# The sums behind the row forms move from the buffer ring "scc" to the ring "ry"

## The chip, the cores and the metric

The kernel runs on one core of one Trainium2 chip. The metric is the device time of one execution in microseconds (us). Of each kernel three plain runs are shown by their median, and one more execution was recorded by the hardware profiler.

## The reference

A two-layer bidirectional encoder trunk over 256 tokens of width 2048, float32. Every layer is a mixer (attention in two parallel head groups and an output projection) and a gated feed-forward network with a short convolution, each behind a normalisation by the root mean square of the row and with a residual. What matters here is the feed-forward part (`D_FF` = 5632, `CONV_W` = 3):

```python
def conv_ffn(x, w_up, conv_w, conv_b, w_down):
    h = jnp.einsum("bsd,df->bsf", x, w_up)
    g, u = h[..., :D_FF], h[..., D_FF:]
    gp = jnp.pad(g, ((0, 0), (1, 1), (0, 0)))
    g = conv_w[0] * gp[:, :-2] + conv_w[1] * gp[:, 1:-1] + conv_w[2] * gp[:, 2:] + conv_b
    return jnp.einsum("bsf,fd->bsd", jax.nn.gelu(g) * u, w_down)
```

## The kernel before

All matrix products run on TensorE with weights streamed from memory in units of 128 x 1024 float32 (`wunit`). A product of float32 precision is made of three products of a reduced format: each operand is split into a high half (a cast on ScalarE, L231) and a low half (source minus high, VectorE, L234), and high x high, high x low and low x high are added up in one PSUM bank (L195, L196, L197). The names `wh` and `wl` are the halves of the weights, `yT` and `prod` the activations of the up and down projections.

The feed-forward network of a layer is done in two halves (`HALVES`): six, then five up blocks (`up_group`), each of 4 x 128 columns of the gate and the same columns of the other factor, and after each half the down projection over the rows that it produced. An up block walks through 8 units of weights for each of two outputs `x`: units 0 to 3 for both outputs by turns, then units 4 to 7 of the one and of the other.

At unit 3 (`UPK`) of each up block, and at three units of each half's down projection (the list `seven`, 1, 2, 3; fewer in the last one), a 2 x 2 block product is done with seven block products instead of eight (a Strassen-Winograd scheme). It needs sums of weight blocks and sums of activation blocks:

- `column_forms` forms the weight sums. `t1` is the first (L951), of ring "rx". `p1` is its split: two tiles, high and low, that are named `form` and, in the up blocks, come from the ring "scc" (L958). The other weights go into the rings of `wh` and `wl`.
- `seven_products` issues seven triples (L977, L978, L979), in the order p21, p22, p11, p3, p1, p2, p4. Four of them go to banks of their own (b1, b5, b6, b7, the tags "s" and "tp"); the triple with p1 goes to b5.
- `extra_parts`, one tick after unit 3, adds those banks up into four tiles named `sum`: `s1` (L844), `x0` (L845), `x1` (L846) and `y1` (L848). `x0` and `x1` come from the ring "ry". L878 adds them to the output at the end of the block.
- `row_forms` forms the activation sums for a down projection from the finished block of activations. It calls `form_sums`, which takes one tile `sums` and writes four sums into it (L324 to L327), and then splits it into `form` tiles. It runs within `multiplied`, for blocks 1, 2, 3 of each half, hence blocks 1, 2, 3 and 7, 8, 9 of each layer.
- `y_forms` forms the activation sums for the up blocks, once a layer, with the same `form_sums`. Its own tile `yf` comes from "ry".

Two orders matter. `multiplied` of a block is put off (`later`) by two ticks, so that in program order it stands in the next up block, behind its unit 1 and ahead of its unit 3. And the framework plans the order of the instructions on each engine itself: it takes what is ready by its own estimate of times, earlier program order first, except where `keep_in_program_order` binds an instruction. A tile of a tag is given out in program order among the tiles of that tag, and an instruction that needs a buffer waits until all readers of the tile that had it are through. The pool `tmp` has two buffers for each tag used here ("scc", "ry", "rx"); all tiles concerned are 128 x 512 float32 or smaller.

Tiles that take buffers in "scc" in the feed-forward network before the change, in program order within an up block: `sums` (where `row_forms` runs), then p1's high half, then p1's low half. In "ry": `x0`, `x1`.

Of the kernel before, what the change touches and what calls it, by code (L numbers as in the profile page):

```python
# [27 lines left out]
F32 = mybir.dt.float32  # L28
# [5 lines left out]
P = 128  # L34
# [37 lines left out]
def trunk_kernel(ctx: ExitStack, tc, a, out):  # L72
# [7 lines left out]
    tmp = ctx.enter_context(tc.tile_pool(name="tmp", bufs=2))  # L80
# [5 lines left out]
    def nm(s):  # L86
        uid[0] += 1
        return f"{s}_{uid[0]}"
# [141 lines left out]
    def split(dst_h, dst_l, src, pin=False):  # L230
        first = S.copy(dst_h, src)  # L231
        if pin:
            tc.keep_in_program_order(first)
        V.tensor_tensor(dst_l, src, dst_h.bitcast(F32), op=ALU.subtract)  # L234
# [70 lines left out]
    def turned_rows(c, gain, res):  # L305

        z = att.tile([P, 2, 512], F32, name=nm("z"), tag="sc", bufs=1)
        V.transpose(z, h[:, :, c * 512:(c + 1) * 512])
        pf = att.tile([P, 8, P], F32, name=nm("hT"), tag="pt", bufs=2)
        moved(z.rearrange("p t k -> p (t k)"), pf)  # L310

        def tiles():
            for j in range(4):
                res[c * 4 + j] = y_tile(pf.rearrange("p (t j) q -> p j t q", t=2)[:, j], gain, c * 4 + j)
            if res is formed.get("of") and c == UPK // 2:
                y_forms(pf.rearrange("p (t j) q -> p j t q", t=2), gain)
        return tiles

    formed = {}

    def form_sums(a11, a21, a12, a22):

        f = tmp.tile([P, 4, P], F32, name=nm("sums"), tag="scc")
        V.tensor_tensor(f[:, 0], a21, a22, op=ALU.add)  # L324
        V.tensor_tensor(f[:, 1], f[:, 0], a11, op=ALU.subtract)
        V.tensor_tensor(f[:, 2], a11, a21, op=ALU.subtract)
        V.tensor_tensor(f[:, 3], a12, f[:, 1], op=ALU.subtract)  # L327
        return f

    def y_forms(src, gain):  # L330

        y = tmp.tile([P, 2, 2, P], F32, name=nm("yf"), tag="ry")
        for k in range(2):
            S.activation(y[:, k], src[:, UPK % 2 * 2 + k], AF.Copy, scale=gain[:, 2 * UPK + k:2 * UPK + k + 1])
        f = form_sums(*(y[:, k, t] for k in range(2) for t in range(2)))
        form = []
        for x, tag in enumerate(("R", "Rq")):
            high = tmp.tile([P, 2, P], F32R, name=nm("form"), tag="t0")
            low = const.tile([P, 2, P], F32R, name=nm("form"), tag=tag, bufs=1)
            split(high, low, f[:, 2 * x:2 * x + 2])  # L340
            form += [(high[:, k], low[:, k]) for k in range(2)]
        formed["form"] = form
# [113 lines left out]
    def qk_tiles(srcs, act, rs, orders, slot):  # L456

        return [qk_sum(ps, r, order, slot + x)
                for x, (ps, r, order) in enumerate(zip(gemm_b(srcs, act), rs, orders))]
# [454 lines left out]

    def row_forms(c4, parts):

        f = form_sums(*(c4[:, 2 + k, t * P:(t + 1) * P] for k in range(2) for t in range(2)))
        form = []
        for high, low in parts:
            n = high.shape[1]  # L920
            split(high, low, f[:, len(form):len(form) + n])
            form += [(high[:, x], low[:, x]) for x in range(n)]
        return form

    def multiplied(j, sides, prod, forms, g0, seven):

        u4, c4 = sides[1], sides[2]
        V.tensor_tensor(c4, c4, u4, op=ALU.mult)
        if j - g0 in seven:
            forms[2 * (j - g0) + 1] = row_forms(c4, new_forms(g0, seven.index(j - g0)))  # L930
        for i in range(4):
            y = new_act("prod", (4 * j + i) % NACT)
            split(y[:, 0, :], y[:, 1, :], c4[:, i, :])
            prod.append(y)
# [223 lines left out]
    for hh in range(2):  # L1158
        vt = v_tiles(gemm_a(a["od_v"][hh], yT, KT), rstd, ((18, 19, 20, 21), (16, 17, 22, 23))[hh])
        for hd in range(hh * 4, hh * 4 + 4):  # L1160
            y = att.tile([P, 6, 64], F32, name=nm("nb"), tag="bias", bufs=2)
# [8 lines left out]
            q, k = qk_tiles([a["od_qk"][hd * 2 + x] for x in range(2)], yT, (Rq, R), (rev, None), hd % 2 * 2)  # L1170
# [236 lines left out]
```

## Time and profile before

| | |
|---|---|
| three runs, median (lowest, highest) | 2412.46 us (2407.63, 2412.59) |
| the profiled execution, its time | 2409.76 us |
| its span, first to last instruction | 2407.9 us |
| mean granted TensorE clock | 0.999 of full speed |
| busy in the span | TensorE matmul 2387.8 us, VectorE 1860.2, ScalarE 1374.0, GpSimd 538.8 |
| HBM read | 458.48 MB |

PE is TensorE's matmuls, PEld its weight loads, DVE VectorE, ACT ScalarE, POOL GpSimd, SP the engine that issues the weight transfers. Rows ordered by time give the start, the duration, the engine, the line, the operation and "output <- inputs" by the names of the tiles, and at the end the number of instructions that the row stands for; a bracket at its end is the idle time of that engine just before, and what ended it. Matmuls are pipelined: one takes 0.39 us, and the next starts about 0.23 us after it did.

### The profile page before, as it was taken

The page shows a single profiled execution, that of the slowest core. Times are in us where ns is not written, and L with a number is a line of the kernel's source. Part 1 is how long each engine was busy: PE and PEld are TensorE (multiplying, and loading weights), DVE is VectorE, ACT ScalarE, POOL GpSimd, SP SyncE. Part 2 cuts the span into 40 slices and gives each one's busy share as a digit, 9 for nine tenths or more (in the row PEclk, how much of TensorE's full clock was granted, in tenths as well). Part 3 has the DMA queues.
Part 4 walks back from the last instruction along what each step waited for, and adds up shares of the span by engine and source line. Part 5 has one row for each costly group of instructions (what it writes and reads, how often), then busy time and mean ns, then how long its engine had stood idle before and what let it go on. Part 6 is the DMA issues. An engine that isn't in the chain of part 4 may idle for free.

```text
span 2407.9 us, 32958 instructions
## 1 busy us (share of the span) xinstructions
PE 2387.8 (99%) x10895; PEld 1982.4 (82%) x10895; DVE 1860.2 (77%) x2461; ACT 1374.0 (57%) x1954; POOL 538.8 (22%) x940
## 2 busy tenths in 40 slices
PE   9999999999999999999999999999999999999998
PEld 7888888888888888888788888888888888888787
DVE  6576567666778888778889868676788887788887
ACT  7455455566656565445656657555565654456564
POOL 1132033322222422004232100422223320033220
PEclk9999999999999999999999999999999999999999
DMA  8778678766777877668777764667778876687874
GB/s 309 203 195 239 196 196 239 216 201 184 218 200 221 213 214 217 202 206 219 213 217 211 221 201 138 193 197 211 201 214 225 208 227 195 207 219 209 236 212 156
DMA packets 287531, 505.64 MB, mean 210 GB/s; under 512 B 159096, under 2 KB 160504, under 8 KB 287360
## 3 DMA queue, kind: packets, MB, share of 16 engines
q1 hardware_dynamic: 256848, 470.15, 65.0%
q0 software_dynamic: 30080, 32.74, 8.0%
q8 instruction: 85, 1.39, 0.2%
q14 instruction: 86, 0.70, 0.1%
q10 hardware_dynamic: 432, 0.66, 0.1%
HBM read 458.48 MB, written 2.18 MB: 191 GB/s over the span
## 4 chain that ended last, share of the span: by engine, by line
PE 45%; DVE 3%; DMA 1%; issue 1%; ACT 1%; SPq 0%; POOL 0%; DVEq 0%; ACTq 0%
PE gm L197 12%; PE gm L196 12%; PE gm L195 12%; PE gm L145 2%; PE gm L150 1%; DVE wl L234 1%; PE gm L978 1%; PE gm L979 1%; PE gm L977 1%; PE tp L978 1%; DVE form L234 1%; DMA qk<-z 1%; ACT wh L231 1%; PE tp L979 0%; PE s L979 0%
## 5 line engine op out<-in xcount | busy, mean ns | idle before, releaser
L231 ACT CAST wh<-raw 128x1024 fp32r<-128x1024 f32 (+1 forms) x897 | 935.7, 1048 | 820.7 <-PE gm L197 651.5
L234 DVE TENSOR_TENSOR wl<-raw,wh 128x1024 fp32r<-128x1024 f32 (+1 forms) x897 | 1085.1, 1216 | 391.3 <-ACT wh L231 384.1
L195 PE MATMUL gm<-wh,yT 128*128 128x512 f32 x2092 | 816.1, 390 | 0.0
L196 PE MATMUL gm<-wl,yT 128*128 128x512 f32 x2092 | 814.7, 389 | 0.3 <-DVE wl L234 0.3
L197 PE MATMUL gm<-wh,yT 128*128 128x512 f32 x2092 | 814.6, 389 | 0.0
L197 PEld LDWEIGHTS gm<-wh,yT 128*128 128x128 f32 x2092 | 392.6, 188 | 82.2 <-DVE yT L240 0.2
L196 PEld LDWEIGHTS gm<-wl,yT 128*128 128x128 f32 x2092 | 392.8, 188 | 81.8 <-DVE wl L234 1.4
L195 PEld LDWEIGHTS gm<-wh,yT 128*128 128x128 f32 x2092 | 392.8, 188 | 80.9 <-ACT junk L265 0.4
L273 POOL DMA_DIRECT2D qk<-sc x264 | 151.7, 583 | 863.9 <-issue 389.6
L273 POOL DMA_DIRECT2D qk<-z x392 | 225.6, 584 | 257.7 <-DVE z L279 227.2
L195 PE MATMUL gm<-wh,prod 128*128 128x512 f32 x518 | 201.5, 389 | 0.0
L197 PE MATMUL gm<-wh,prod 128*128 128x512 f32 x518 | 201.5, 389 | 0.0
L196 PE MATMUL gm<-wl,prod 128*128 128x512 f32 x518 | 201.5, 389 | 0.0
L195 PEld LDWEIGHTS gm<-wh,prod 128*128 128x128 f32 x518 | 97.2, 188 | 20.3
L196 PEld LDWEIGHTS gm<-wl,prod 128*128 128x128 f32 x518 | 97.2, 188 | 20.2
L197 PEld LDWEIGHTS gm<-wh,prod 128*128 128x128 f32 x518 | 97.2, 188 | 20.2
L196 PE MATMUL gm<-wl,mix 128*128 128x512 f32 x256 | 100.1, 391 | 0.9 <-DVE wl L234 0.9
L195 PE MATMUL gm<-wh,mix 128*128 128x512 f32 x256 | 100.0, 391 | 0.0
L197 PE MATMUL gm<-wh,mix 128*128 128x512 f32 x256 | 99.6, 390 | 0.0
L273 POOL DMA_DIRECT2D hT<-z x72 | 41.4, 583 | 199.8 <-PE gm L197 75.5
L856 ACT ACTIVATE sum<-sum,rstd 128x512 f32<-128x512 f32 x88 | 59.7, 718 | 17.7 <-DVE sum L845 10.0
L145 PE MATMUL gm<-yT,wh 128*128 128x512 f32 x256 | 59.5, 390 | 0.0
(356 smaller groups left out, 2644.1 us busy)
## 6 DMA issues: line engine op xcount, KB each, us to landing
raw<-in_up SPq DMA_DIRECT2D x352, 512.0 KB, 4.5
raw<-in_down SPq DMA_DIRECT2D x176, 512.0 KB, 4.4
raw<-in_eva_qk SPq DMA_DIRECT2D x96, 512.0 KB, 4.3
raw<-in_eva_v SPq DMA_DIRECT2D x46, 512.0 KB, 6.0
raw<-in_evb_qk SPq DMA_DIRECT2D x32, 512.0 KB, 4.7
raw<-in_ev_out SPq DMA_DIRECT2D x32, 512.0 KB, 4.3
raw<-in_od_qk SPq DMA_DIRECT2D x32, 512.0 KB, 4.3
raw<-in_od_out SPq DMA_DIRECT2D x32, 512.0 KB, 4.3
```

Of the source, the lines that this page charges most:

```text
L145: T.matmul(ps.rearrange("p a b -> p (a b)"), wh[:, k * P:(k + 1) * P], act[u * 8 + k].rearrange("p a b -> p (a b)"), start=(u == 0 and k = ...
L150: T.matmul(ps[:, 1, :], wl[:, k * P:(k + 1) * P], act[u * 8 + k][:, 0, :], start=False, stop=(u * 8 + k == KT - 1))
L195: T.matmul(ps[t], ah, wh[:, sl], start=(kt == 0), stop=False)
L196: T.matmul(ps[t], ah, wl[:, sl], start=False, stop=False)
L197: T.matmul(ps[t], al, wh[:, sl], start=False, stop=(kt == nk - 1))
L231: first = S.copy(dst_h, src)
L234: V.tensor_tensor(dst_l, src, dst_h.bitcast(F32), op=ALU.subtract)
L273: (nc.sync if i in on_sync else G).dma_start(dst[j * 32:(j + 1) * 32, :, i * 32:(i + 1) * 32], z[i * 32:(i + 1) * 32].rearrange("p (b j c) ...
L856: S.activation(sums[x][t], sums[x][t], AF.Copy, scale=rstd[0][:, t:t + 1])
L977: T.matmul(ps, ah, wh, start=own and first, stop=False)
L978: T.matmul(ps, ah, wl, start=False, stop=False)
L979: T.matmul(ps, al, wh, start=False, stop=own and last)
```

## The change

`form_sums` gets the ring as an argument. `y_forms` passes "scc" as before; `row_forms` passes "ry", so that its `sums` tile takes a buffer from the ring of `x0` and `x1` and not from that of p1. The rest of the code is the same.

```diff
-    def form_sums(a11, a21, a12, a22):
+    def form_sums(tag, a11, a21, a12, a22):
 
-        f = tmp.tile([P, 4, P], F32, name=nm("sums"), tag="scc")
+        f = tmp.tile([P, 4, P], F32, name=nm("sums"), tag=tag)
...
     def y_forms(src, gain):
...
-        f = form_sums(*(y[:, k, t] for k in range(2) for t in range(2)))
+        f = form_sums("scc", *(y[:, k, t] for k in range(2) for t in range(2)))
...
     def row_forms(c4, parts):
 
-        f = form_sums(*(c4[:, 2 + k, t * P:(t + 1) * P] for k in range(2) for t in range(2)))
+        f = form_sums("ry", *(c4[:, 2 + k, t * P:(t + 1) * P] for k in range(2) for t in range(2)))
```

## The prediction

> **What bounds the kernel now.** I read the page first, then the table of waits for TensorE, then the time-ordered lists of TensorE, VectorE and ScalarE around one up block that stalls and one that doesn't.
>
> ```profile
> span 2407.9 us, 32958 instructions
> PE 2387.8 (99%) x10895; PEld 1982.4 (82%) x10895; DVE 1860.2 (77%) x2461; ACT 1374.0 (57%) x1954; POOL 538.8 (22%) x940
> ```
>
> TensorE (PE) sets the time: only 2407.9 - 2387.8 = 20.1 us of the span is not matmul. A change that touches no matmul can win only what TensorE waits for. The waits of TensorE (total us, times, longest):
>
> ```profile
> PE tp L978 <- DVE form L234: 8.0, 11, 1.2
> PE gm L196 <- DVE wl L234: 1.2, 2, 0.9
> ```
>
> The first row is the change's place. L978 is the second product of a triple in `seven_products`; "tp <- form" is the fifth triple, whose weight is `p1`, the split of `t1`. TensorE waits 11 times for the low half of p1 (`form` by L234, VectorE). Now the same stretch in a block that doesn't wait (block 1 of layer 0):
>
> ```profile
> 720.65 0.39 PE L977 MATMUL gm<-wh,yT 128*128 128x512 f32 x1
> 723.39 0.40 PE L977 MATMUL tp<-form,form 128*128 128x512 f32 x1
> 723.63 0.39 PE L978 MATMUL tp<-form,form 128*128 128x512 f32 x1
> 723.86 0.40 PE L979 MATMUL tp<-form,form 128*128 128x512 f32 x1
> 725.70 0.39 PE L196 MATMUL gm<-wl,yT 128*128 128x512 f32 x1
> 728.19 0.39 PE L195 MATMUL gm<-wh,yT 128*128 128x512 f32 x1
> ```
>
> and in the next block, which waits:
>
> ```profile
> 763.55 0.39 PE L977 MATMUL gm<-wh,yT 128*128 128x512 f32 x1
> 766.30 0.40 PE L977 MATMUL tp<-form,form 128*128 128x512 f32 x1
> 767.91 0.39 PE L195 MATMUL gm<-wh,yT 128*128 128x512 f32 x1
> 769.35 0.49 PE L978 MATMUL tp<-form,form 128*128 128x512 f32 x1 [1.05 <-DVE form L234]
> 769.68 0.39 PE L979 MATMUL tp<-form,form 128*128 128x512 f32 x1
> 769.91 0.39 PE L196 MATMUL gm<-wl,yT 128*128 128x512 f32 x1
> 772.43 0.39 PE L195 MATMUL gm<-wh,yT 128*128 128x512 f32 x1
> ```
>
> From the first L977 to the last row stand 33 matmuls in both. The undisturbed block takes 728.19 - 720.65 = 7.54 us (0.229 a matmul), the other 772.43 - 763.55 = 8.88. So the stall costs 1.33 us, more than the 1.05 of the wait table, because matmuls overlap and the pipe must fill again. In the bad block the written order has already put seven other matmuls between L977 and L978 of p1, and TensorE still waits.
>
> Where p1 is made. VectorE and ScalarE (ACT) in the undisturbed block:
>
> ```profile
> 711.24 0.61 ACT L231 CAST form<-t 128x512 fp32r<-128x512 f32 x1
> 715.75 0.69 DVE L234 TENSOR_TENSOR form<-t,form 128x512 fp32r<-128x512 f32 x1
> ```
>
> and in the stalled one:
>
> ```profile
> 746.94 1.40 DVE L878 SCALAR_TENSOR_TENSOR z<-gm,rstd,sum 128x512 f32<-128x512 f32 x2
> 752.01 0.69 DVE L951 TENSOR_TENSOR t<-raw 128x512 f32<-128x512 f32 x1 [1.28 <-DMA raw<-in_up]
> 764.65 0.28 DVE L324 TENSOR_TENSOR sums<-qk 128x128 f32<-128x128 f32 x1
> 767.14 0.42 DVE L234 TENSOR_TENSOR form<-sums,form 128x256 fp32r<-128x256 f32 x1
> 767.48 1.22 DVE L234 TENSOR_TENSOR wl<-raw,wh 128x1024 fp32r<-128x1024 f32 x1
> 768.61 0.68 DVE L234 TENSOR_TENSOR form<-t,form 128x512 fp32r<-128x512 f32 x1
> 769.21 0.68 DVE L845 TENSOR_TENSOR sum<-sum,tp 128x512 f32<-128x512 f32 x1
> 770.94 0.68 DVE L846 TENSOR_TENSOR sum<-sum,s 128x512 f32<-128x512 f32 x1
> ```
> ```profile
> 761.42 1.05 ACT L231 CAST wh<-raw 128x1024 fp32r<-128x1024 f32 x1 [1.55 <-DVE raw L955]
> 763.64 1.33 ACT L231 CAST prod<-qk 128x256 fp32r<-128x256 f32 x4 [1.16 <-DVE qk L928]
> 764.87 0.62 ACT L231 CAST form<-t 128x512 fp32r<-128x512 f32 x1
> ```
>
> Undisturbed, p1's halves are written 9.4 and 4.9 us before the seven products start. In the stalled block `t` is there at 752.70, yet p1's high half is cast at 764.87, 1.3 us after the start, although ScalarE stood idle 1.55 and 1.16 us before that. It comes right behind the first write of `sums` (L324, 764.65), and p1's low half at 768.61, behind the last reader of `sums` (767.14 + 0.42). That is the picture of ring "scc": two buffers, and `sums`, p1 high, p1 low ask for them in this order. p1 high can't take its buffer before `sums` took one, and p1 low takes the one that `sums` gives up. The same picture stands in exactly 12 of the 22 up blocks: those behind blocks 1, 2, 3, 7, 8, 9 of each layer, where `row_forms` runs. The other 10 show no wait.
>
> The loss of each of the 12 by the count of 33 matmuls (8.88 us in the first, 9.56 in the last, whose rows follow, each less 7.545): 1.33, 1.24, 1.07, 1.04, 0.66, 0.84, 0.50, 0.40, 1.55, 0.88, 0.70, 2.02. Sum **12.2 us**, the ceiling (the last holds TensorE's 0.3 us wait for `wl` there too).
>
> ```profile
> 2266.24 0.39 PE L977 MATMUL gm<-wh,yT 128*128 128x512 f32 x1
> 2275.80 0.40 PE L195 MATMUL gm<-wh,yT 128*128 128x512 f32 x1
> ```
>
> **The change part by part.** No instruction, byte or DMA is added or removed; no queue (SP, POOL) gets another step. Three dependences change.
>
> 1. p1 no longer shares a ring with `sums`. Its buffers were last read by the previous block's fifth triple (723.86 + 0.40 in the pair above), some 28 us before it wants them. So p1 can be made as in the undisturbed blocks, and TensorE's wait goes: at most 12.2 us.
>
> 2. `sums` now waits for a buffer of "ry", held by the two sums x0 and x1 of the previous `extra_parts` until L878 has read them. L878 ends at 746.94 + 1.40 = 748.34, `sums` is first written at 764.65: 16 us to spare. Cost 0.
>
> 3. x1 (written by L846) now waits until `sums` is read out. That is at 767.56, L846 starts at 770.94: 3.4 us to spare. Cost 0. If that cover went, VectorE would stand at L846 with the next low weights queued behind it; TensorE would wait for those.
>
> What is late next. ScalarE's cast (0.62) moves into its idle time. VectorE's part of p1 moves ahead of the row-form work, and there VectorE is full:
>
> ```profile
> 720.65:728.20 7.55, 7.55 (x35) 6.20 (x34) 7.51 (x11) 6.16 (x10) 0.00 (x0) 1.00 0.78 226
> 763.55:771.10 7.55, 6.50 (x29) 5.02 (x28) 7.55 (x17) 7.37 (x13) 0.00 (x0) 1.00 0.62 176
> ```
>
> (columns: PE, PEld, VectorE, ScalarE busy us; VectorE 7.55 of 7.55.) So everything from there to the first unit behind the seven products (call it U4) moves back by p1 low's share, 0.60 us (768.61 to 769.21), unless VectorE had an idle gap. U4's low weights are wanted 22 matmuls after the start, 5.02 us (725.70 - 720.65 = 5.05 undisturbed). They end now at 5.15 us in the first stalled block (767.48 + 1.22 - 763.55) and 4.98 in the last; in the others between 3.37 and 4.85. With 0.60 added they overrun 5.02 by 0.73, 0.43, 0.09, 0.25 and 0.56 us in five of the 12 blocks, in sum 2.06; with VectorE's gaps just before (0.55 in the second of these, 0.17 in the fourth) about 1.5. Each such wait also refills the pipe: L978 to L979 above took 0.33 where 0.23 is usual, 0.1 apiece, 0.5. So I take 2.0 us as left. Low end: nothing but the 0.13 of the first block is left, if p1 low finds gaps everywhere. High end: the split of `sums`, which in eight blocks stands behind U4's low weights, goes ahead of them because ScalarE reaches its cast 0.5 us sooner; a further 0.60 in those blocks makes 3.9, with refills 4.7. In the last block:
>
> ```profile
> 2270.00 1.22 DVE L234 TENSOR_TENSOR wl<-raw,wh 128x1024 fp32r<-128x1024 f32 x1
> 2271.13 0.69 DVE L234 TENSOR_TENSOR form<-sums,form 128x512 fp32r<-128x512 f32 x1
> ```
>
> Sum: 12.2 - 2.0 = **10.2 us** gained, between 7.5 and 12.1. Against the profiled execution's 2409.76 (span 2407.9 and 1.86 around it) that is 2399.6. The median of the three runs, 2412.46, stands 2.7 above that execution, so I forecast 2402.3 (0.42% faster); the runs themselves spread over 5 us, which is also why 0.2%, 4.8 us, is about what a measurement can tell.
>
> **A rule weighed.** The two rows of stretches above (7.51 of 7.55 and 7.55 of 7.55) say that VectorE has no room there. The Trainium skill, Perfetto Trace Analysis, Identifying Performance Opportunities, says that a kernel generally improves by improving its most-contended engine. VectorE gets no less work here, so by that sentence the stall would stay and the time with it, 2412. The trace speaks against it: in all 12 blocks the late instruction is one whose input was ready about 12 us before (752.70 against 764.87 above), and the undisturbed block has as full a VectorE (7.51 of 7.55) and no wait. That VectorE is full I have charged as the 2.0 us.
>
> **The rivals.**
> - The gain is handed over: VectorE's backlog is worse than the sum says (0.15 to 0.2 us in each of the 12 blocks beyond the high end above, as by `prod` splits in another order). 12.2 - 4.7 less 1.8 to 2.4 leaves 5 to 6 us: 2407. Against it: the ten undisturbed blocks keep U4 ahead.
> - Nothing changes: p1's place is set by the written order, not by the ring, and the new order leaves it behind the row forms; or VectorE's work, not a buffer, is the bound, and the wait only changes its name. Time 2412. For it: VectorE is full. Against it: ScalarE's idle 1.55 and 1.16 us while p1's input lay ready.
> - Slower: x0 and x1 (L845, L846) are written ahead of U4's low weights. They stand before them in program order. x0 needs the sixth triple, which starts 15 matmuls in and ends at about 17 x 0.229 + 0.39 = 4.3 us; then x0 and x1 (0.60 each) and the low weights (1.22) end at 6.7, 1.7 us past 5.02, where the average loss now is 1.0. In 12 blocks 12 x 1.7 - 12.2 = 8 us slower: 2420.7. x0 alone ahead gives 1.1 us a block, no change; it decides from the second sum on. Against it: in every up block of this trace L845 stands behind U4's low weights (767.48 before 769.21 above).
>
> **How the numbers follow.** The forecast (gain 7.5 to 12.2) gets 0.72, handed over 0.10, no change 0.11 (0.07 by the written order, 0.04 by VectorE's work), slower 0.07. Faster by over 0.2% is the first two, 0.82. The lowest run less the ceiling, 2407.6 - 12.2 = 2395.4, is the low end; with handed over at 2407 and a run's spread the range reaches to 2408, and leaves out about 0.2. The likeliest case's own range is 2395.4 to 2405.
>
> **What would show it.** Right: the row "PE tp L978 <- DVE form" is gone; in all 12 blocks p1 low is written 4 to 5 us before the first L977, and L977, L978, L979 of p1 run in a row; the 33 matmuls take 7.5 us except in the first and last block of a half, where "PE gm L196 <- DVE wl" shows some 0.5 us; L846 shows no wait. Wrong: p1's cast still behind the prod casts; or new waits of L196 that add up to several us; or L845 before U4's low weights.

## The result and the profile after

| | before | after |
|---|---|---|
| median of five runs (lowest to highest) | 2412.46 us (2407.63 to 2413.59) | 2402.37 us (2400.53 to 2403.41) |
| the profiled execution | 2409.76 us | 2402.49 us |
| its span | 2407.9 us | 2400.6 us |

The ratio after to before is 0.996, with a 95% interval of 0.9945 to 0.9974: faster. The medians differ by 10.1 us, the two profiled executions by 7.3. The forecast of 2402.3 lies so near partly by luck: it was a gain of 10.2 taken off a median that stood 2.7 above its own profiled execution, and after the change the profiled execution stands at the median. In the later comparisons the median of the kernel before was 2410.0 and 2409.9 us; a forecast made from those would have been 2399.8.

What TensorE waited for, after (total us, times, longest):

```profile
PE gm L196 <- DVE wl L234: 2.5, 5, 0.9
PE tp L978 <- DVE wl L234: 0.6, 1, 0.6
```

The row "PE tp L978 <- DVE form L234: 8.0, 11" is gone. L196 waits 2.5 us where it waited 1.2: 1.3 us of it in three of the 12 blocks (0.3 before), the rest in the mixer of layer 1. The block whose loss was 1.33 us, VectorE's rows after (in order of time):

```profile
752.37 0.69 DVE L951 TENSOR_TENSOR t<-raw 128x512 f32<-128x512 f32 x1 [1.51 <-DMA raw<-in_up]
760.14 0.69 DVE L234 TENSOR_TENSOR form<-t,form 128x512 fp32r<-128x512 f32 x1
765.49 0.28 DVE L324 TENSOR_TENSOR sums<-qk 128x128 f32<-128x128 f32 x1
767.30 0.75 DVE L234 TENSOR_TENSOR form<-sums,form 128x256 fp32r<-128x256 f32 x2
768.31 2.35 DVE L234 TENSOR_TENSOR wl<-raw,wh 128x1024 fp32r<-128x1024 f32 x2
770.58 0.68 DVE L845 TENSOR_TENSOR sum<-sum,tp 128x512 f32<-128x512 f32 x1
772.32 0.68 DVE L846 TENSOR_TENSOR sum<-sum,s 128x512 f32<-128x512 f32 x1
```

and TensorE's:

```profile
763.68 0.39 PE L977 MATMUL gm<-wh,yT 128*128 128x512 f32 x1
766.43 0.40 PE L977 MATMUL tp<-form,form 128*128 128x512 f32 x1
766.66 0.39 PE L978 MATMUL tp<-form,form 128*128 128x512 f32 x1
766.89 0.40 PE L979 MATMUL tp<-form,form 128*128 128x512 f32 x1
769.58 0.50 PE L196 MATMUL gm<-wl,yT 128*128 128x512 f32 x1 [0.68 <-DVE wl L234]
```

p1's low half is written 3.5 us before the first L977, where it was written 5.1 us after it, and p1's triple runs in a row. ScalarE's cast moved with it:

```profile
756.00 0.62 ACT L231 CAST form<-t 128x512 fp32r<-128x512 f32 x1
```

That is 7.7 us before the first L977 (1.3 after it, before the change). L845 and L846 show no wait: x1 got its buffer in "ry" without a stop. But the next unit's low weights (U4) end at 768.31 + 1.22 = 769.53, 5.85 us after the first L977, wanted at 5.02, so TensorE stops there: this block still loses 1.03 us.

Over all 12 blocks, what 33 matmuls take above the 7.545 us of an undisturbed block, the excess, is 3.3 us in sum (12.2 before). Five blocks of the 12 have none: the second, the fourth, the fifth, the ninth and the tenth. The largest are the first (1.03) and the last (0.75). So the blocks gave 8.9 us in the profiled executions, and the span 7.3: 0.9 came back in the down projection of layer 0's first half (the L978 row above, a wait for p2's low half), 0.6 between the last block of layer 0 and the first of layer 1, and 0.1 ahead of the first block.

### The profile page after: what moved, and what is told of

It is laid out like the page before. It is cut to its first block, busy times and chain, and to the rows that moved or that the text cites. A ratio compares the mean times of both kernels' runs of the same rounds, so it can differ in the third digit from the quotient of the medians.

```text
span 2400.6 us, 32954 instructions
## 1 busy us (share of the span) xinstructions
PE 2386.9 (99%) x10895; PEld 1983.1 (83%) x10895; DVE 1859.8 (77%) x2461; ACT 1374.5 (57%) x1954; POOL 539.7 (22%) x940
## 4 chain that ended last, share of the span: by engine, by line
PE 59%; DVE 3%; DMA 2%; issue 1%; POOL 1%; ACT 1%; SPq 1%; DVEq 0%; ACTq 0%; POOLq 0%
PE gm L196 16%; PE gm L197 16%; PE gm L195 16%; PE gm L145 2%; DVE wl L234 1%; PE gm L978 1%; PE gm L979 1%; PE gm L977 1%; POOL qk L273 1%; PE gm L150 1%; DMA qk<-z 1%; PE tp L978 1%; PE tp L979 1%; PE tp L977 1%; PE s L978 1%
## 5 line engine op out<-in xcount | busy, mean ns | idle before, releaser
L234 DVE TENSOR_TENSOR wl<-raw,wh 128x1024 fp32r<-128x1024 f32 (+1 forms) x897 | 1083.3, 1215 | 383.7 <-ACT wh L231 373.0
L196 PE MATMUL gm<-wl,yT 128*128 128x512 f32 x2092 | 815.6, 390 | 2.3 <-DVE wl L234 2.2
L196 PEld LDWEIGHTS gm<-wl,yT 128*128 128x128 f32 x2092 | 392.9, 188 | 86.2 <-DVE wl L234 6.3
L196 PE MATMUL gm<-wl,prod 128*128 128x512 f32 x518 | 201.5, 389 | 0.0
L196 PEld LDWEIGHTS gm<-wl,prod 128*128 128x128 f32 x518 | 97.3, 188 | 20.2
L196 PE MATMUL gm<-wl,mix 128*128 128x512 f32 x256 | 100.1, 391 | 0.4 <-DVE wl L234 0.4
```

Of the source, the lines that this page charges most:

```text
L196: T.matmul(ps[t], ah, wl[:, sl], start=False, stop=False)
```

## The experiments

All compare with the kernel before on the same chip. "Excess" is the sum over the 12 blocks, as above, of one profiled execution each.

| kernel | sums in | median, us | ratio (95%) | excess |
|---|---|---|---|---|
| before | "scc" | 2412.5, 2410.0, 2409.9 | 1 | 12.2 |
| after | "ry" | 2402.4 | 0.9960 (0.9945 to 0.9974) | 3.3 |
| own ring | a buffer of their own | 2402.2 | 0.9966 (0.9953 to 0.9978) | 4.7 |
| low apart | "scc", p1's low half elsewhere | 2409.3 | 0.9995 (0.9985 to 1.0004) | 9.7 |
| late, "scc" | "scc", put off by three ticks | 2398.3 | 0.9952 (0.9939 to 0.9964) | 0.04 |
| late, "ry" | "ry", put off by three ticks | 2400.1 | 0.9958 (0.9945 to 0.9970) | 0.3 |
| twice | "ry", written twice | 2407.7 | 0.9990 (0.9982 to 0.9999) | 8.0 |
| late twice | "scc", put off, written twice | 2400.8 | 0.9965 (0.9953 to 0.9978) | 0.95 |
| layer 0 | "ry" in layer 0 alone | 2404.8 | 0.9980 (0.9971 to 0.9989) | 7.4 |

The three numbers for before are those of the three comparisons: the change, the first four experiments, the last three.

**A buffer of their own.** Does sharing "ry" with x0 and x1 cost anything?

```diff
-        f = tmp.tile([P, 4, P], F32, name=nm("sums"), tag=tag)
+        f = tmp.tile([P, 4, P], F32, name=nm("sums"), tag=tag, bufs=1 if tag == "junk" else 2)
...
-        f = form_sums("ry", *(c4[:, 2 + k, t * P:(t + 1) * P] for k in range(2) for t in range(2)))
+        f = form_sums("junk", *(c4[:, 2 + k, t * P:(t + 1) * P] for k in range(2) for t in range(2)))
```

> The kernel after, but the sums of the row forms take neither ring: they get the one buffer of the tag 'junk', which nothing else uses in the up blocks. The written order on every engine is the same as in the kernel after. Theory (what helped is that p1's halves no longer queue behind the sums; the ring 'ry' costs nothing): the same as the kernel after, 10 us faster than before (0.996), 33-matmul excess over the 12 blocks 3.3 us as there. Rival (sharing 'ry' with x0 and x1 holds VectorE at L846 and makes part of the 3.3 us that are left): 1 to 3 us faster than the kernel after, excess under 2 us.

2402.2 us, the kernel after's median to 0.2 us; by the ratios 0.9966 against 0.9960, with intervals that overlap. "ry" costs nothing that can be measured. The excess is 4.7 us and not 3.3, with the same written order on every engine: the residue differs by over a microsecond from one execution to the next, so a single profile's excess is good to about that.

**p1's low half apart.** Is it the buffer that the sums hold, or that p1 asks for its buffers behind them?

```diff
-            p1, = apart([tmp.tile([P, 512], F32R, name=nm("form"), tag="scc") for _ in range(2)], t1)
+            p1, = apart([tmp.tile([P, 512], F32R, name=nm("form"), tag=x, bufs=n) for x, n in (("scc", 2), ("junk", 1))], t1)
```

> The kernel before (sums in 'scc'), but p1's low half alone gets the buffer of 'junk'. So p1's low half no longer needs the buffer that the sums give up, while p1's high half still asks for its buffer behind the sums. Theory with two parts (order of asking and the buffer itself): the high half stays late, cast about 1 us after the first L977; the low half follows the product splits, ahead of the next unit's low weights. The first and fourth kind of block gains nearly nothing, the others about half: excess 12.2 to about 6.5 us, time about 5.5 us under before. Rival (only the buffer that the sums hold counts): about the kernel after, excess 3 to 4 us, 9 to 10 us under before. Rival (only the place of the high half counts): excess stays at 11 to 12, time as before.

2409.3 us, ratio 0.9995: no change that can be told, excess 9.7. The time agrees with the rival that only the high half's place counts, the excess lies between it and the theory. ScalarE, VectorE and TensorE in the first of the 12 blocks (first L977 at 762.95):

```profile
763.06 1.33 ACT L231 CAST prod<-qk 128x256 fp32r<-128x256 f32 x4 [1.16 <-DVE qk L928]
764.29 0.62 ACT L231 CAST form<-t 128x512 fp32r<-128x512 f32 x1
```
```profile
764.08 0.28 DVE L324 TENSOR_TENSOR sums<-qk 128x128 f32<-128x128 f32 x1
766.89 0.69 DVE L234 TENSOR_TENSOR form<-t,form 128x512 fp32r<-128x512 f32 x1
```
```profile
767.64 0.50 PE L978 MATMUL tp<-form,form 128*128 128x512 f32 x1 [1.10 <-DVE form L234]
```

The high half still stands behind L324, though its own buffer is free and no longer shared with a later tile: it is the turn in the ring, not the buffer, that holds it. And then the low half, late on a full VectorE, comes 1.1 us too late again. Of the 8.9 us of excess that the change took away, freeing the low half alone gives 2.5. I had expected more: I took TensorE to ask for the low half behind p2 and p4 in eight blocks, as in the kernel before; in this kernel it asks right behind the high half in those eight. The reverse, the high half alone apart, was not run.

**The sums put off.** If the turn in the ring is the cause, then letting p1 ask first must help without any other ring; and if VectorE's backlog makes the residue (the 3.3 us that are left after the change), that must go too.

```diff
         if j - g0 in seven:
-            forms[2 * (j - g0) + 1] = row_forms(c4, new_forms(g0, seven.index(j - g0)))
+            later(3, lambda: forms.update({2 * (j - g0) + 1: row_forms(c4, new_forms(g0, seven.index(j - g0)))}))
```

> The kernel before, sums still in 'scc', but the row forms are put off by three more ticks, so that they stand in program order behind the same block's p1 and behind the first two units after it. Theory (order within the ring, and VectorE's backlog for what is left): p1 is made 4 to 5 us ahead as in the undisturbed blocks, the 1.4 us of sums and their split no longer stand ahead of the next unit's low weights, the excess falls from 12.2 to under 0.5 us, the time to 11 to 13 us under before, 1 to 3 us better than the kernel after. Rival (a planner's accident, or the ring 'ry' itself helps): excess stays near 12, time as before. Rival (the residue of 3.3 us does not come from the sums ahead of those weights): excess 2 to 4, as the kernel after.

2398.3 us, 0.9952, excess 0.04. The waits of TensorE (whole span) hold no row of p1, and L196 waits 0.6 us in all:

```profile
PE s L475 <- DVE sc L759: 0.8, 1, 0.8
PE gm L196 <- DVE wl L234: 0.6, 1, 0.6
```

VectorE in its first of the 12 blocks (first L977 at 763.16):

```profile
759.61 0.69 DVE L234 TENSOR_TENSOR form<-t,form 128x512 fp32r<-128x512 f32 x1
764.97 1.43 DVE L234 TENSOR_TENSOR prod<-qk,prod 128x256 fp32r<-128x256 f32 x4
766.31 2.35 DVE L234 TENSOR_TENSOR wl<-raw,wh 128x1024 fp32r<-128x1024 f32 x2
768.58 0.29 DVE L324 TENSOR_TENSOR sums<-qk 128x128 f32<-128x128 f32 x1
```

p1 is early with the sums still in "scc"; U4's low weights end at 767.53, 4.4 us after the first L977, in time; the sums follow. The stretch of 33 matmuls (the columns as in the prediction) beside the same one of the kernel after:

```profile
763.16:770.71 7.55, 7.55 (x34) 6.20 (x33) 7.51 (x15) 6.70 (x12) 0.00 (x0) 1.00 0.68 214
```
```profile
763.68:771.23 7.55, 6.87 (x30) 5.32 (x29) 7.51 (x16) 6.86 (x12) 0.00 (x0) 1.00 0.52 149
```

VectorE is as full in the one as in the other, 7.51 of 7.55 us, and TensorE stops in one only.

The same with the sums in "ry":

> The kernel after (sums in 'ry'), with the row forms put off by three more ticks. There the sums come behind x0 and x1 in the ring and wait until L878 has read them, 14 us later. Theory (VectorE's backlog ahead of the next unit's low weights is what is left): excess under 0.5 us, 11 to 13 us under before, 1 to 3 us better than the kernel after. Rival: the later sums hold the activations' buffer longer and stall the next convolution on ScalarE and VectorE; then new waits of L196 on the low weights near the end of the block, no better than the kernel after.

2400.1 us, excess 0.3, nearly all of it in the last block. No new wait of the convolution shows on TensorE. Against the version in "scc" the medians differ by 1.8 us, within what the intervals leave open.

**The sums written twice.** The residue by dose: 0.8 us of VectorE more in each block, ahead of U4's low weights (in the kernel after) or behind them (in the version put off).

```diff
+        for _ in range(2 if tag == "ry" else 1):
-        V.tensor_tensor(f[:, 0], a21, a22, op=ALU.add)
+            V.tensor_tensor(f[:, 0], a21, a22, op=ALU.add)
...
```

> The kernel after, with the four sums of every row form written twice over: 0.8 us more of VectorE (4 x 0.20) in each of the 12 blocks, ahead of the next unit's low weights. Theory (what is left of the stall is those weights coming late behind VectorE's backlog): they end now at 4.7 to 5.9 us after the first L977 and are wanted at 5.0; with 0.8 more every one of the 12 is late, the excess goes from 3.3 to about 12 us, on the row of L196 waiting for wl (8 to 10 us of it), the time back to within 2 us of before. p1 stays 4 us early. Rival (the residue has another cause, a transfer or ScalarE): excess stays at 3 to 6 us, time 6 to 10 us under before.

2407.7 us, 0.999: all but 2 us of the gain is lost again. The excess is 8.0 us. The waits, over the whole span:

```profile
PE gm L196 <- DVE wl L234: 6.7, 8, 1.9
PE tp L978 <- DVE wl L234: 1.9, 1, 1.9
```

Of the first row 5.5 us lie in seven of the 12 blocks and 1.3 in the mixer of layer 1; the second row lies in the last down projection. Expected were 12 us of excess over all 12 blocks. But the longer sums also changed the written order: in eight blocks of this kernel U4's low weights stand ahead of the split of the sums (together 2.8 us of excess). In the four where the split stayed ahead (the first, fourth, seventh and tenth) the excess is 5.2 us against 1.2 in the same four of the kernel after: 1.0 more a block on average where 0.8 was added, but 0.2, 2.3, 1.0 and 0.5 singly. The fourth block shows that the added work is not all: its transfer kept L951 waiting 1.91 us, where the kernel after waits 0.02 (the last section comes back to this):

```profile
1137.32 0.69 DVE L951 TENSOR_TENSOR t<-raw 128x512 f32<-128x512 f32 x1 [1.91 <-DMA raw<-in_up]
1154.12 1.22 DVE L234 TENSOR_TENSOR wl<-raw,wh 128x1024 fp32r<-128x1024 f32 x1
```
```profile
1155.39 0.50 PE L196 MATMUL gm<-wl,yT 128*128 128x512 f32 x1 [1.95 <-DVE wl L234]
```

> The same doubling in the kernel with the row forms put off by three ticks and the sums in 'scc': the same extra 0.8 us of VectorE in each of the 12 blocks, behind the weights. Theory (place, not amount, of VectorE's work decides): excess stays under 1 us, time as with the row forms put off and written once, 11 to 13 us under before. Rival (VectorE's amount of work in these blocks is the bound): 5 to 9 us of it come back.

2400.8 us, 0.9965; excess 0.95, nearly all of it in the last block. In the other eleven blocks the same work costs the 33 matmuls nothing when it stands behind the weights. In the last block, too, U4's low weights end (2262.44) before the doubled sums begin (2263.49), so its excess is not theirs. The median is still 2.5 us above the version written once, with intervals that overlap; that is less than the 5 to 9 of the rival but not nothing. By the profiled executions (spans 2398.6 and 2395.1 us) 0.9 of the 3.6 us is the last block's excess, 1.4 lies behind it to the end, 0.7 ahead of the first block and 0.6 between the layers. Of this only a second wait of L196 in the last block, 0.5 us, 12 us after its first L977, is seen behind doubled sums; why the rest differs stays open.

**Layer 0 alone.**

```diff
-        f = form_sums("ry", *(c4[:, 2 + k, t * P:(t + 1) * P] for k in range(2) for t in range(2)))
+        f = form_sums("scc" if formed["layer"] else "ry", *(c4[:, 2 + k, t * P:(t + 1) * P] for k in range(2) for t in range(2)))
...
-        rstd, res = [], None
+        rstd, res, formed["layer"] = [], None, layer
```

> The kernel before in layer 1, the kernel after in layer 0: the sums take 'ry' in layer 0 alone. Theory: the six blocks of layer 0 have an excess of 1 to 2.5 us (6.2 before), the six of layer 1 keep 6.0, with L978 waiting for p1 in them; time 4 to 5 us under before (0.998). Rival (the gain is not local to the blocks, or hangs on one layer's neighbourhood): 0 or 10 us under before.

2404.8 us, 0.998, as expected. The excess is 1.5 us in layer 0 and 5.9 in layer 1 (6.2 and 6.0 before). The waits of TensorE in the feed-forward part of layer 0, then of layer 1 up to 2300 us (behind that, in the last down projection, L978 waits 1.5 us for p2's low half):

```profile
PE gm L196 <- DVE wl L234: 0.9, 1, 0.9
```
```profile
PE tp L978 <- DVE form L234: 3.5, 4, 1.1
PE gm L196 <- DVE wl L234: 0.4, 1, 0.4
```

The gain is made in the blocks where `row_forms` runs, and each layer has its half.

## Why the prediction was right, point by point

- **The cause.** Right, and shown: with the sums out of "scc" (own ring), or behind p1 in it (put off), p1 is made early, as in the ten undisturbed blocks, and the wait is gone; the gain follows the layer. Of the two halves of the argument, the buffer that the sums give up to p1's low half isn't enough by itself: freeing the low half alone left the time where it was, with the high half still behind the sums. What the high half's turn is worth alone was not run.
- **The ceiling, 12.2 us.** Right: the version with an excess of 0.04 stands 11.7 us under the median before, and 12.8 by the profiled spans.
- **"Cost 0" for both waits in "ry".** Right: the same time as with a buffer of their own, and L846 shows no wait.
- **What is late next.** The mechanism is right and its size was too small. I took 2.0 us as left, from bounds of 0.13 and 4.7; the profiles show 3.3 and 4.7 for the same written order. The step that fell short is the choice between the ends: I charged p1's 0.60 us alone, which made five blocks late, and left the split of the sums ahead of U4's low weights to the high end. In the trace before it stood behind them in eight of the twelve blocks; after, it stands ahead of them in all twelve, as in the second one (first L977 at 807.61):

```profile
810.64 0.68 DVE L234 TENSOR_TENSOR form<-sums,form 128x512 fp32r<-128x512 f32 x1
811.24 2.35 DVE L234 TENSOR_TENSOR wl<-raw,wh 128x1024 fp32r<-128x1024 f32 x2
```

  So the order was that of the high end. Two of the signs came out otherwise as well: p1's low half is written 3.5 to 5.0 us before the first L977 (forecast 4 to 5), and the excess isn't confined to the first and last block of a half. The eighth and eleventh of the 12 lose 0.49 and 0.38, the fourth, ninth and tenth nothing.
- **Where the rest went.** Not foreseen: 1.6 us that the blocks had gained were given back outside them. The largest part, 0.9 us, goes with the wait of L978 for p2's low half in the down projection of layer 0's first half. Such a wait stands in the same place with p1's low half apart (1.2 us), and in the last down projection with the sums written twice (1.9) and with "ry" in layer 0 alone (1.5). Two of these waits come where the sums are in "scc", so "ry" isn't needed for it; the kernel before and the other versions don't show it. What decides it stays open.
- **The sentence on the most-contended engine** in the Trainium skill's Perfetto Trace Analysis, Identifying Performance Opportunities: taken as the prediction took it, with VectorE as the engine to improve because the stretch is full, it did not hold here. It may not be the right reading: over the span TensorE is the fuller one (matmuls 99%, weight loads 82%, VectorE 77%), and what the change took away were waits of TensorE. VectorE's busy time is 1860.2 us before and 1859.8 after, it is as full in the stretch (7.51 of 7.55), and the kernel gained 0.4%. The doubled sums cost 2.5 us in the version put off and 5.3 in the kernel after by the medians (3.1 and 7.2 by the ratios; the intervals of the first pair overlap), in excess 0.9 and 4.7. What counts here is what stands ahead of the instruction that TensorE waits for.
- **The rivals.** Slower, by x0 and x1 ahead of U4's low weights: not seen, L845 stands behind them in all 12 blocks (768.31 before 770.58 in the first). No change by the written order: the order moved as the ring let it.

## What to carry to other kernels

When an instruction is late whose input lay ready long before, on an engine that stood idle meanwhile, look at who else takes buffers of its tag: tiles of a tag are given out in program order, and a late tile holds up an early one behind it, even where a buffer is free. Either give the late tile another ring, or let it ask later; where the engine is full the second also moves the late tile's work behind what the bound engine wants next. Here that took the excess to 0.04 us against 3.3; the times, 0.9952 against 0.9960, have overlapping intervals and don't tell the two apart. And before crediting a removed wait in full, add up what stands ahead of the next thing that the bound engine needs.

## What had not been expected

With the same instructions in the same order, the excess differed between two executions of different placement by 1.4 us (3.3 and 4.7), and single blocks by up to 0.64 (0.21 and 0.85 us for the seventh). The transfer that ends VectorE's idle time ahead of such a block lands at another time in each trace: L951 waits 1.51 us for it in the kernel after and 1.03 with the sums in a buffer of their own:

```profile
751.59 0.69 DVE L951 TENSOR_TENSOR t<-raw 128x512 f32<-128x512 f32 x1 [1.03 <-DMA raw<-in_up]
```

That first block's excess is 1.03 us in the one and 0.52 in the other, and VectorE's list ran full behind that transfer in both. The other blocks fit the pair. In the 24 blocks of these two traces, the ten in which L951 waits 0.7 us or more lose 0.2 to 1.0 us, each within 0.1 us of its wait less 0.5. Of the other 14 nine lose at most 0.05; the five that lose more show a later idle time of VectorE instead, in four of them for the transfer qk<-z (0.71 to 1.41 us, at L928 or L897). The fourth block with the sums written twice, 1.91 us of waiting and 2.28 of excess, has both the late transfer and the 0.8 us of added work. With the sums put off in "ry" L951 waits up to 1.67 us, and those blocks lose nothing. So the residue goes with two things together: a transfer that lands late, and sums that stand ahead of U4's low weights. When a transfer lands was not varied by itself, and what sets it stays open.
